# A hybrid convolution layer in Strassen-Winograd products: opening reordered, weight sums moved to VectorE, pools split by tile kind, and a rewritten end

## The chip, the cores and the metric

The kernel runs on one core of a Trainium2 chip, as one launch. Its metric is the device time of that launch in microseconds (us). TensorE (PE) multiplies matrices, VectorE (DVE) and ScalarE (ACT) work element by element, GpSimd (POOL) does so too, and SyncE (SP) issues most transfers; ACT issues some.

## The reference, cut to what matters

DEPTH is 1, so there is one layer, with the convolution mixer, on x of 2048 rows by 1024 columns, in fp32:

```python
c_act = jax.nn.silu(c)
mod = c_act @ ada_w[0] + ada_b[0]
sh_m, sc_m, g_m, sh_f, sc_f, g_f = jnp.split(mod, 6, axis=-1)
h = rms_norm(x, norm_gains[0, 0]) * (1 + sc_m) + sh_m
gate_b, gate_c, v = jnp.split(h @ conv_w_in[0], 3, axis=-1)
h = (gate_b * causal_conv3(gate_c * v, conv_w[0])) @ conv_w_out[0]
x = x + g_m * rms_norm(h, norm_gains[0, 1])
h = rms_norm(x, norm_gains[0, 2]) * (1 + sc_f) + sh_f
g, u = jnp.split(h @ ffn_w_gate_up[0], 2, axis=-1)
h = (jax.nn.silu(g) * u) @ ffn_w_down[0]
out = x + g_f * rms_norm(h, norm_gains[0, 3])
```

`rms_norm` divides a row by the root of its mean square and multiplies by a gain; 1024 is the width of the model and 2816 that of the feed-forward part.

## The kernel before, in words

Features lie on the 128 partitions and tokens along the free axis, in tiles of 128 x 512. The tokens are cut into two units of 1024, each of two halves of 512. Eight phases follow one another: in0, out0, in1, out1, gu0, down0, gu1, down1 (the digit is the unit). In each, matrix products are done in 2 x 2 blocks by Strassen-Winograd with seven products, P1 to P7, instead of eight. A product's operands are sums of blocks: of features, A11, A12, A22, S1 to S4; of weights, as `Blocks.sum` (L317) forms them. Every operand of a product is split into an upper part ("high": a cast to fp32r on ACT) and a lower part ("low": a subtraction on DVE), and one 128 x 512 step of a product is three matmuls: high weight by high feature, low weight by high feature, high weight by low feature. In the trace in0A11h and in0A11l are the high and low part of feature operand A11 of phase in0, in1b is a raw weight block of its weight group 1, in1P a weight operand, and in0P, as an output, a PSUM bank.

Nothing is scheduled by a planner. Every call goes through `Engine.emit` (L75), which keeps each engine's instructions in the order in which they are written, so all rows of the trace carry L75. The bulk of the program is a list of slots (one slot is one operand pair on PE); `schedule(slot, f)` and `later(slots, f)` put the other work between slots. `advance(step, n)` carries the weight preparation (loading blocks, summing them, casting high, forming low) up to product n. The first nine slots are not run from that list but written out by hand in `start()`, the **opening**:

- x arrives as rows (`xr`, four tiles of 128 x 1024 per half of 512 tokens) and, transposed, as features in four tiles a, c, b, d (a and b belong to token half 0, c and d to half 1; a and c hold feature blocks 0 to 3, b and d blocks 4 to 7).
- `squares` (L1009): ACT squares the rows and sums them up; `factor` (L1016): v on DVE, the power on POOL (r0p, r1p), three small DVE operations, four that build a diagonal (r0d, r1d); `spread` (L236): one PE matmul puts the factor on all partitions (r0b, r1b), ACT copies it to SBUF (r0r, r1r).
- `mult` (DVE) multiplies a feature tile by r, `shift` (ACT) applies scale mA and shift mB. For column pair q, mA comes from `scales` (DVE products of ada rows with c) and mB from `shifts` (16 PE matmuls into a row pms), `turned` (an ACT copy of the row and two PE transposes) and `fold` (four tiny DVE operations).
- `upper` and `lower` make the high and low parts, `products` issues the matmuls, `follow` the evictions from PSUM.

The products of the opening stand in the order A11 (P1), S3 (P7), A12 (P2), S2 (P6), S1 (P5), with weight groups 0, 1 and 2 in each. The features S3 need c, A12 needs b, S2 needs d.

The **end** is the second half of tokens of down1: `ready_z` (L607) is called as each of eight output tiles z is finished; `add_square` adds its squares to an accumulator (down1q). `after_down` (L875) normalises the first half and writes it, tile by tile: z becomes z times the gate mG times the factor, is added to x (tile xo) and stored. `last_half` (L920) does so for the second half, after the last matmul: PE sums the squares over the partitions (lasts), DVE and POOL take the root (lastv, lastp, lastt, lastq), DVE builds the diagonal (lastd), PE spreads it (lastb), ACT copies it (lastr), and DVE does five tiles and POOL three (5, 6, 7, scaled by mG ahead on ACT); SP stores them (tiles xl).

Of the kernel before, what the change touches and what calls it, by code (L numbers as in the profile page):

```python
# [10 lines left out]
F32 = mybir.dt.float32  # L11
F32R = mybir.dt.float32r
AF = mybir.ActivationFunctionType
ALU = mybir.AluOpType
# [32 lines left out]
def hybrid_conv_layer(  # L47
# [34 lines left out]
    sb = ctx.enter_context(tc.tile_pool(name="sb", bufs=1))  # L82
# [3 lines left out]
    def big(name, dt=F32):  # L86
        return sb.tile([P, 4, CH], dt, tag="big", bufs=NBIG, name=name)

    def raw(name):
        return sb.tile([P, CH], F32, tag="raw", bufs=NRAW, name=name)  # L90

    def pair(name):
        return sb.tile([P, 2, CH], F32, tag="wp", bufs=NWP, name=name)
# [42 lines left out]
    vt = const.tile([P, 112], F32, name="vt")  # L136
# [107 lines left out]
    def spread_later(q, name, put):  # L244
        dg = diagonal(q, name)
        yield 4
        put(spread(dg, name))
# [53 lines left out]
    class Blocks:  # L301
# [15 lines left out]
        def sum(self, op):  # L317
            b = self.b
            if op in ("P7", "P6") and "T3" not in self.summed:
                self.summed.add("T3")  # L320
                E = V if self.kind == "in" and self.opening else G
# [174 lines left out]
    class Group:  # L496
# [119 lines left out]
        def ready_z(self, c):  # L616
# [5 lines left out]
            add_square(ph.acc, tok, z, f"{ph.name}q{tok}{n}", V if ph.last and c == "21" else G, 0.5 if ph.last else 1)  # L622
            ph.tiles_done[tok] += 1
            ph.tile_ready(tok, n, z)
# [251 lines left out]
    def after_down(ph, tok):  # L876
# [10 lines left out]
        yield from spread_later(q, f"o{u}{tok}", partial(put, rb, 0))  # L887
# [16 lines left out]
        for k in range(KD):  # L904
# [6 lines left out]
            yield 2  # L911
# [4 lines left out]
    POOLS = (5, 6, 7)  # L916

    def last_half(ph):

        u, tok = ph.u, 1  # L920
        st = bank("lasts")
        for t in range(4):
            PE.matmul(st[:, t : t + 1], ph.acc[tok][:, t * P : (t + 1) * P], mean, start=True, stop=True)
        v = small(4, "lastv")
        V.tensor_scalar(v, st[:, :4], EPS, None, ALU.add)
        dg = diagonal(at_once(root(v, "last")), "last")
        b = bank("lastb")
        PE.matmul(b, one, dg[:, :CH], start=True, stop=True)
        rb = sb.tile([P, CH], F32, tag="rb", bufs=NRB, name="lastr")
        A.copy(rb, b)  # L930
        mine = [k for k in range(KD) if k not in POOLS]
        for n in range(len(mine)):
            if n < len(POOLS):
                k = POOLS[n]
                z, xt = ph.z(tok, k), ph.xt[k]
                G.tensor_tensor(z, z, rb, ALU.mult)
                G.tensor_tensor(xt, xt, z, ALU.add)
            k = mine[n]
# [4 lines left out]
        for k in POOLS:  # L943
            SP.dma_start(out_tile(u, tok, k), ph.xt[k])
        yield

    def before_last(ph):
# [4 lines left out]
        yield 1  # L952
        for k in POOLS:
            z = ph.z(1, k)
            A.activation(z, z, AF.Copy, scale=col(mG[1], k))
# [25 lines left out]
    def start():  # L981
# [34 lines left out]
        def factor(tok):  # L1016
            v = small(4, f"v{tok}")
            V.tensor_scalar(v, sq[tok], EPS, None, ALU.add)
            return diagonal(at_once(root(v, f"r{tok}")), f"r{tok}")
# [49 lines left out]
        for h in range(2):  # L1069
            A.activation(c_half[h], c_half[h], AF.Silu)  # L1070
# [4 lines left out]
        advance("blocks", 2)  # L1075
        load_scale(1)
        load_shift(1)
        load_rows(1)
# [11 lines left out]
        squares(0, range(4))  # L1090
        dg = factor(0)
# [3 lines left out]
        shifts(0)  # L1095
        for k in range(4):
            mult("a", k)
        advance("high", 2)
        turned(0)
        advance("low", 2)  # L1100
        scales(1, 0)
# [211 lines left out]
```

## Time and profile before

| | us |
|---|---|
| device time, three runs | 2041.07, 2039.4, 2040.47 |
| their median | 2040.47 |
| device time of the profiled execution | 2041.43 |
| span of the profiled execution | 2039.3 |

| engine | busy us | share of the span |
|---|---|---|
| PE | 1941.7 | 95% |
| DVE | 1444.0 | 71% |
| ACT | 855.2 | 42% |
| POOL | 691.1 | 34% |

The span is the time from the first to the last event of the profiled execution; its device time is 2.13 us more. The shares are averages over the whole span; in the page's 40 slices of 51 us each, PE is at five tenths in the first and the last, at seven in the second, and at eight or nine in all others. PE's mean granted clock over the span is 0.982 of its full 2.4 GHz; it has one other level, half of it, 1.2 GHz. Times in the trace count from the start of the span.

### The profile page before, as it was taken

The numbers are of one execution on the slowest core, as the hardware profiler recorded it, in microseconds if no ns is written. First come the engines' busy times: TensorE is split into PE (matmuls) and PEld (weight loads), VectorE is DVE, ScalarE is ACT, GpSimd is POOL, SyncE is SP. The second block draws the span as 40 slices with busy tenths as digits, with TensorE's granted clock in tenths as the row PEclk, the third lists the DMA queues.
The fourth block names the chain that finished last, engine by engine and source line by source line (L and its number), as shares of the span: only waits on it lengthen the run. The fifth ranks groups of instructions, "written<-read, shape, count | busy, mean of one in ns | idle before, by whom it ended". The sixth has DMA issues, their size and how long they took to land.

```text
span 2039.3 us, 25010 instructions
## 1 busy us (share of the span) xinstructions
PE 1941.7 (95%) x8432; PEld 1578.8 (77%) x8432; DVE 1444.0 (71%) x1878; ACT 855.2 (42%) x1382; POOL 691.1 (34%) x451
## 2 busy tenths in 40 slices
PE   5799998999989899999999999999999999999995
PEld 2578886778767778887888888887888888888884
DVE  4887887886989685699767656667767455465465
ACT  5443355632333663343333445544333333344451
POOL 0324541301542133357856431111443343311022
PEclk9899999999999999999999999999999999999998
DMA  9259959879766875477656788567646234285544
GB/s 382 74 205 352 358 203 327 322 266 347 243 212 206 300 258 175 151 232 257 224 186 218 256 280 308 196 249 258 222 162 220 94 127 132 67 326 208 203 145 136
DMA packets 206193, 463.19 MB, mean 227 GB/s; under 512 B 23024, under 2 KB 38512, under 8 KB 199152
## 3 DMA queue, kind: packets, MB, share of 16 engines
q1 hardware_dynamic: 179136, 397.49, 56.9%
q10 hardware_dynamic: 26928, 64.10, 8.3%
q8 instruction: 66, 1.08, 0.2%
q14 instruction: 63, 0.52, 0.1%
HBM read 328.33 MB, written 133.17 MB: 226 GB/s over the span
## 4 chain that ended last, share of the span: by engine, by line
PE 70%; DVE 13%; DMA 8%; ACT 4%; issue 3%; POOL 1%; SPq 0%; ACTq 0%; DVEq 0%; POOLq 0%
PE gu1P L75 20%; PE gu0P L75 16%; PE down1P L75 10%; PE down0P L75 10%; PE in0P L75 6%; PE in1P L75 5%; PE out1P L75 2%; DMA xx<-xt_d 1%; PE out0P L75 1%; DVE ada L75 1%; DMA xr<-x_d 1%; DVE zz L75 1%; DMA kgu1P<-gu1P 1%; DVE in0y L75 1%; DMA x<-xx 1%
## 5 line engine op out<-in xcount | busy, mean ns | idle before, releaser
L75 DVE TENSOR_TENSOR gu1a<-gu1P,gu1a 128x512 f32<-128x512 f32 x63 | 43.4, 690 | 93.0 <-PE gu1P L75 86.2
L75 DVE TENSOR_TENSOR gu0a<-gu0P,gu0a 128x512 f32<-128x512 f32 x63 | 43.2, 687 | 59.5 <-PE gu0P L75 54.0
L75 POOL TENSOR_TENSOR down0q<-down0q,down0q 128x512 f32<-128x512 f32 x14 | 26.0, 1859 | 152.3 <-ACT down0q L75 152.2
L75 POOL TENSOR_TENSOR down1q<-down1q,down1q 128x512 f32<-128x512 f32 x10 | 16.2, 1618 | 147.0 <-ACT down1q L75 147.0
L75 DVE CUSTOM_DVE_ANT_0 ada<-ada,c 128x512 f32<-128x512 f32 x80 | 62.5, 791 | 0.2 <-ACT c L75 0.2
L75 ACT COPY gu1a<-gu1P 128x512 f32<-128x512 f32 x42 | 24.5, 587 | 89.7 <-PE gu1P L75 78.1
L75 ACT COPY gu0a<-gu0P 128x512 f32<-128x512 f32 x42 | 24.5, 584 | 73.4 <-PE gu0P L75 65.9
L75 ACT COPY gu1g<-gu1P 128x512 f32<-128x512 f32 x24 | 14.1, 588 | 90.7 <-PE gu1P L75 85.9
L75 POOL TENSOR_TENSOR gu1a<-gu1a 128x512 f32<-128x512 f32 x11 | 19.5, 1776 | 89.8 <-DVE gu1g21s L75 24.7
L75 DVE TENSOR_TENSOR gu1g<-gu1P,gu1g 128x512 f32<-128x512 f32 x24 | 16.6, 691 | 44.9 <-ACT gu1g L75 43.6
L75 POOL TENSOR_TENSOR nq<-nq,nq 128x512 f32<-128x512 f32 x28 | 45.7, 1630 | 3.0 <-ACT nq L75 2.8
L75 ACT COPY gu0g<-gu0P 128x512 f32<-128x512 f32 x24 | 14.1, 586 | 72.6 <-PE gu0P L75 72.6
L75 POOL TENSOR_TENSOR out1q<-out1q,out1q 128x512 f32<-128x512 f32 x14 | 24.2, 1726 | 58.5 <-ACT out1q L75 58.4
L75 DVE TENSOR_TENSOR xx<-xx,zz 128x512 f32<-128x512 f32 x32 | 35.9, 1121 | 5.4 <-DMA xx<-xt_d 4.4
L75 DVE TENSOR_TENSOR gu0g<-gu0P,gu0g 128x512 f32<-128x512 f32 x24 | 16.6, 690 | 31.8 <-ACT gu0g L75 31.3
L75 POOL TENSOR_TENSOR out0q<-out0q,out0q 128x512 f32<-128x512 f32 x14 | 24.7, 1764 | 42.4 <-ACT out0q L75 42.3
L75 POOL TENSOR_TENSOR in0b<-in0b,in0b 128x512 f32<-128x512 f32 x7 | 10.7, 1533 | 79.4 <-DVE in1y L75 37.3
L75 POOL TENSOR_TENSOR gu0a<-gu0a 128x512 f32<-128x512 f32 x11 | 19.5, 1777 | 48.3 <-DVE gu0g11s L75 8.0
L75 ACT ACTIVATE gu1a<-gu1a 128x512 f32<-128x512 f32 x42 | 26.5, 633 | 15.0 <-DVE xo L75 7.7
L75 ACT ACTIVATE nq<-xx 128x512 f32<-128x512 f32 x32 | 20.2, 631 | 28.9 <-DVE xx L75 24.7
L75 ACT ACTIVATE gu0a<-gu0a 128x512 f32<-128x512 f32 x42 | 26.6, 633 | 13.5 <-DVE gu0a L75 12.2
L75 DVE TENSOR_TENSOR down2P<-down2P,down2P 128x512 fp32r<-128x512 f32 x14 | 11.1, 795 | 28.6 <-ACT down2P L75 28.6
(3209 smaller groups left out, 7014.8 us busy)
## 6 DMA issues: line engine op xcount, KB each, us to landing
ada<-ada_d SPq DMA_DIRECT2D x64, 256.0 KB, 5.2
act0A<-gu0a SPq DMA_DIRECT2D x33, 256.0 KB, 4.1
act1A<-gu1a SPq DMA_DIRECT2D x33, 256.0 KB, 3.2
ada<-ada_d SPq DMA_DIRECT2D x16, 512.0 KB, 8.9
zz<-z SPq DMA_DIRECT2D x32, 256.0 KB, 4.2
xx<-xt_d SPq DMA_DIRECT2D x32, 256.0 KB, 4.4
x<-xx ACTq DMA_DIRECT2D x32, 256.0 KB, 3.9
down0S<-act0S SPq DMA_DIRECT2D x8, 1024.0 KB, 7.4
```

What stands on the lines that cost most here:

```text
L75: return tc.keep_in_program_order(f(*args, **kwargs))
```

## The change

The change has three parts.

1. **Pools.** The pool `sb` becomes four: `bigs` (tiles of 128 x 2048), `pairs`, `raws` (128 x 512) and `sb` for the rest, and the constant `vt` is padded from 112 to 136 columns. In the allocation every tile of the first three kinds now begins, in its partition, at an address that is a multiple of 256 bytes; before, these addresses were 64 above such a multiple.
2. **Opening.** The squares of the first half of rows stand ahead of c's two activations on ACT. The rows of the second half are loaded ahead of scale and shift 1; their squares are spread (one tile before `turned(0)`, one after `fold(0)`, two after A11's first two tiles). A11's products of k = 0, 1 come before `shifts(1)`; the second factor's matmul and copy (r1b, r1r) before `turned(1)`, `fold(1)` and before A11's k = 2, 3. `scales(1, 1)` stands between POOL's power and the operations that need it. `shifts(2)` moves from before c to behind S3's products of k = 0, 1, with `turned(2)` and `shifts(3)` behind all of S3's. P7's third weight group is cast before c. A12's products are cut in two. All nine weight sums of P6 and P5 move from POOL to DVE; S1 is formed tile by tile in `start()`, and the steps of S4 and A22 are scheduled a slot earlier.
3. **End.** The last tile's square is not added to the accumulator; PE sums both (four more matmuls). All eight tiles z are scaled by mG ahead on ACT. x of five tiles (4, 5, 6, 7, 0) is put into PSUM by PE with the identity as the other operand, two tiles before the sums of squares and three after; when z has been multiplied by lastb (DVE), PE adds z into the same bank, ACT copies the sum out and issues the store. For tiles 1, 2, 3 DVE multiplies and adds. lastr and POOL's share go. The first half of tokens is written out at a closer pace (1.5 slots a tile for 2, two slots of lag for 4).

```diff
-    sb = ctx.enter_context(tc.tile_pool(name="sb", bufs=1))
+    bigs, pairs, raws, sb = (ctx.enter_context(tc.tile_pool(name=n, bufs=1)) for n in ("bigs", "pairs", "raws", "sb"))
...
         def sum(self, op):
-            b = self.b
+            b, E = self.b, V if self.opening else G
...
             if op == "P6":
-                G.tensor_tensor(b["11+"], b["12"], b["11+"], ALU.add)
+                E.tensor_tensor(b["11+"], b["12"], b["11+"], ALU.add)
             if op == "P5":
-                G.tensor_tensor(b["21"], b["21"], b["11+"], ALU.subtract)
-                G.tensor_tensor(b["11+"], b["22"], b["11+"], ALU.subtract)
+                E.tensor_tensor(b["21"], b["21"], b["11+"], ALU.subtract)
+                E.tensor_tensor(b["11+"], b["22"], b["11+"], ALU.subtract)
...
+            if ph.last and ph.tiles_done[1] == KD:
+                ph.sq = tmp("lastq")
+                A.activation(ph.sq[:, :CH], z, AF.Square)
+                scaled_z()
...
+        for k in ON_PE[:2]:
+            add_x(k)
+        for i, sq in enumerate((ph.acc[tok], ph.sq)):
+            for t in range(4):
+                PE.matmul(col(st, 4 * i + t), sq[:, t * P : (t + 1) * P], mean, start=True, stop=True)
+        for k in ON_PE[2:]:
+            add_x(k)
...
+        for k in ON_PE + tuple(k for k in range(KD) if k not in ON_PE):
             z, xt = ph.z(tok, k), ph.xt[k]
-            V.scalar_tensor_tensor(z, z, col(mG[1], k), b, ALU.mult, ALU.mult)
-            V.tensor_tensor(xt, xt, z, ALU.add)
-            SP.dma_start(out_tile(u, tok, k), xt)
...
+            V.tensor_tensor(z, z, b, ALU.mult)
+            if k in ON_PE:
+                PE.matmul(sums[k], ident, z, start=False, stop=True, skip_group_check=True)
+                A.copy(xt, sums[k])
+                A.dma_start(out_tile(u, tok, k), xt)
+            else:
+                V.tensor_tensor(xt, xt, z, ALU.add)
+                SP.dma_start(out_tile(u, tok, k), xt)
...
         squares(0, range(4))
+        for h in range(2):
+            A.activation(c_half[h], c_half[h], AF.Silu)
...
         products(0, range(2))
-        dg = factor(1)
+        scales(1, 0)
+        dg = factor(1, partial(scales, 1, 1))
+        shifts(1)
+        ps_ = bank("r1b")
+        PE.matmul(ps_, one, dg[:, :CH], start=True, stop=True)
+        turned(1)
+        rb[1] = sb.tile([P, CH], F32, tag="rb", bufs=NRB, name="r1r")
+        A.copy(rb[1], ps_)
+        fold(1)
...
         advance("sums", 5)
-        advance("high", 4)
-        rb[1] = spread(dg, "r1")
+        advance("high", 5)
...
-        shifts(2)
...
         products(3, range(2))
+        shifts(2)
+        products(3, range(2, 4))
+        turned(2)
         shifts(3)
-        products(3, range(2, 3))
-        turned(2)
-        products(3, range(3, 4))
...
-        advance("sums", 11)
         advance("high", 8)
```

On PE, between the first factor's shift row and the last A11 products, before (in0P_0, in0P_1, in0P_2 are the PSUM banks of the three weight groups; pms is the shift row, r1b the second factor spread over the partitions):

```order
MATMUL pms_262<-ada_1_158,cact 1x256 x8
MATMUL pms_262<-ident,ada_1_158 128x1 x2
MATMUL in0P_0_294<-in0A11h,in0P_243 128x512 x2
...
MATMUL in0P_2_302<-in0A11l,in2P_247 128x512
MATMUL r1b<-r1d,one 128x512
MATMUL pms_365<-ada_2_181,cact 1x256 x8
MATMUL in0P_0_401<-in0S3h,in0P_356 128x512 x2
```

and now:

```order
MATMUL in0P_2_290<-in0A11l,in2P_252 128x512
MATMUL pms_321<-ada_1_171,cact 1x256 x8
MATMUL r1b<-r1d,one 128x512
MATMUL pms_321<-ident,ada_1_171 128x1 x2
MATMUL in0P_0_282<-in0A11h,in0P_248 128x512 x2
...
MATMUL in0P_2_290<-in0A11l,in2P_252 128x512
MATMUL in0P_0_401<-in0S3h,in0P_369 128x512 x2
```

The second factor has moved from behind all 36 matmuls of A11 to behind 18 of them, with the shift row of pair 1; the shift row of pair 2 (pms with ada_2) no longer stands ahead of S3.

On DVE, from the multiplication of d to the last low part of S2, before (in0P from in0b is a low part of P6's weights; in0c and in0C there are evictions of PSUM):

```order
TENSOR_TENSOR in0d<-in0d,r1r 128x512 x4
TENSOR_TENSOR in0a<-in0d,in0e 128x512 x4
TENSOR_TENSOR in0c_11_452<-in0P_0_515,in0c_11_452 128x512
TENSOR_TENSOR in0C_11_454<-in0P_1_519,in0C_11_454 128x512
TENSOR_TENSOR in0P_543<-in0b_462,in0P_543 128x512
TENSOR_TENSOR in0S2l<-in0a,in0S2h 128x512
TENSOR_TENSOR in1P_547<-in1b_465,in1P_547 128x512
TENSOR_TENSOR in0S2l<-in0a,in0S2h 128x512
TENSOR_TENSOR in2P_551<-in2b_468,in2P_551 128x512
TENSOR_TENSOR in0S2l<-in0a,in0S2h 128x512 x2
```

and now, with P6's three sums ahead of d and P5's six behind S1's additions:

```order
TENSOR_TENSOR in0b_541<-in0b_176,in0b_541 128x512
TENSOR_TENSOR in1b_544<-in1b_180,in1b_544 128x512
TENSOR_TENSOR in2b_547<-in2b_184,in2b_547 128x512
TENSOR_TENSOR in0d<-in0d,r1r 128x512 x4
...
TENSOR_TENSOR in0S2l<-in0a,in0S2h 128x512 x2
TENSOR_TENSOR in0b_11_465<-in0P_2_560,in0b_11_465 128x512
TENSOR_TENSOR in0c<-in0c,in0d 128x512 x4
TENSOR_TENSOR in0b_199<-in0b_199,in0b_541 128x512
TENSOR_TENSOR in0b_541<-in0b_178,in0b_541 128x512
...
TENSOR_TENSOR in0S1l<-in0c,in0S1h 128x512 x4
```

The nine sums stand on DVE's queue, and none is left on POOL's.

On PE at the end, before, behind the last product (lasts are the sums of squares, lastb the factor spread out):

```order
MATMUL lasts<-mean,down1q_15761 128x1 x4
MATMUL lastb<-lastd,one 128x512
```

and now:

```order
MATMUL lastx_16080<-xl_15845,ident 128x512
MATMUL lastx_16082<-xl_15847,ident 128x512
MATMUL lasts<-mean,down1q_15787 128x1 x4
MATMUL lasts<-mean,lastq 128x1 x4
MATMUL lastx_16092<-xl_15849,ident 128x512
MATMUL lastx_16094<-xl_15851,ident 128x512
MATMUL lastx_16096<-xl_15837,ident 128x512
MATMUL lastb<-lastd,one 128x512
MATMUL lastx_16080<-down1z_15312,ident 128x512
...
MATMUL lastx_16096<-down1z_15100,ident 128x512
```

Ten matmuls with the identity have come in, two of them ahead of the sums of squares.

## Rows read from the trace of the kernel before

**Rows 1.** Busy time by stretch, core 0: us, busy and instructions by engine, clock, DMA.

```profile
31.50:43.10 11.60, 11.60 (x43) 8.53 (x43) 4.70 (x14) 6.29 (x11) 1.01 (x1) 0.85 1.03 399
43.10:54.10 11.00, 8.02 (x27) 4.19 (x26) 9.32 (x16) 6.58 (x12) 0.00 (x0) 0.79 1.02 407
...
74.05:91.50 17.45, 11.19 (x39) 7.78 (x39) 16.59 (x20) 8.41 (x14) 8.10 (x5) 0.89 0.00 0
...
138.00:200.00 62.00, 62.00 (x274) 51.29 (x274) 46.65 (x59) 22.00 (x38) 27.62 (x20) 1.00 0.97 361
```

**Rows 2.** Timeline, 7 to 45 us: start, duration, engine, operation, wait before it.

```profile
9.93 0.43 SPq L75 DMA_DIRECT2D in0a<-xt_d  x1
...
13.22 1.04 ACT L75 ACTIVATE xr<-xr 128x1024 f32<-128x1024 f32 x1
...
14.38 0.17 DVE L75 TENSOR_SCALAR v<-a 128x4 f32<-128x4 f32 x1 [9.53 <-ACT xr L75]
...
19.95 2.50 DVE L75 TENSOR_TENSOR in0a<-in0a,r0r 128x512 f32<-128x512 f32 x4 [0.34 <-ACT r0r L75]
```

**Rows 3.** Transfers issued in 2.05 to 2.7 us: count, KB each, median us to landing.

```profile
xr<-x_d SPq DMA_DIRECT2D x2, 512.0 KB, 8.0
```

**Rows 4.** Transfers issued in 0 to 60 us: count, KB each, median us to landing.

```profile
in0a<-xt_d SPq DMA_DIRECT2D x1, 1024.0 KB, 8.4
```

**Rows 5.** Chain of waits, 0 to 115 us: start, duration, engine and its work.

```profile
31.56 10.04 PE in0P L75 x36
...
43.11 0.70 DVE in0c L75
```

**Rows 6.** Timeline of PE, 42 to 64 us.

```profile
41.43 1.02 PE L75 MATMUL r1b<-r1d,one 128*128 128x512 f32 x2
...
56.52 3.61 PE L75 MATMUL pms<-ada,cact 128*1 128x256 f32 x16
```

**Rows 7.** Timeline of DVE, 43 to 110 us.

```profile
50.90 0.69 DVE L75 TENSOR_TENSOR in2P<-in2b,in2P 128x512 fp32r<-128x512 f32 x1 [1.31 <-ACT in2P L75]
...
52.71 1.46 DVE L75 TENSOR_TENSOR in0S3l<-in0e,in0S3h 128x512 fp32r<-128x512 f32 x2
...
58.82 1.75 DVE L75 TENSOR_TENSOR in2P<-in2b,in2P 128x512 fp32r<-128x512 f32 x1
60.49 1.24 DVE L75 TENSOR_TENSOR mf<-ms,ms 128x2 f32<-128x2 f32 x1
...
63.15 2.49 DVE L75 TENSOR_TENSOR in0b<-in0b,r0r 128x512 f32<-128x512 f32 x4
...
74.05 2.49 DVE L75 TENSOR_TENSOR in0d<-in0d,r1r 128x512 f32<-128x512 f32 x4
...
87.39 3.44 DVE L75 TENSOR_TENSOR in0S2l<-in0a,in0S2h 128x512 fp32r<-128x512 f32 x2
```

**Rows 8.** Groups of POOL's instructions, 54 to 92 us: busy us, mean ns of one.

```profile
L75 POOL TENSOR_TENSOR in2b<-in2b,in2b 128x512 f32<-128x512 f32 x3 | 5.0, 1683 | 0.1
```

**Rows 9.** What PE waited for, 40 to 140 us: total us, times, longest.

```profile
PE in0P L75 <- DVE in0S4l L75: 1.4, 1, 1.4
```

**Rows 10.** Timeline of all engines, 2014 to 2040 us.

```profile
2015.38 0.69 DVE L75 TENSOR_TENSOR down1z<-down1P,down1z 128x512 f32<-128x512 f32 x1 [3.95 <-PE down1P L75]
...
2017.51 1.05 PE L75 MATMUL lasts<-mean,down1q 128*128 128x1 f32 x8 [2.17 <-DVE down1q L75]
...
2021.56 2.07 PE L75 MATMUL lastb<-lastd,one 128*128 128x512 f32 x2 [3.00 <-DVE lastd L75]
...
2024.29 0.75 DVE L75 SCALAR_TENSOR_TENSOR down1z<-down1z,mG,lastb 128x512 f32<-128x512 f32 x1 [2.78 <-ACT lastr L75]
...
2034.54 0.69 DVE L75 TENSOR_TENSOR xo<-xo,down1z 128x512 f32<-128x512 f32 x1
```

**Rows 11.** Busy time by stretch at the end, as in Rows 1.

```profile
2018.97:2024.30 5.33, 2.07 (x2) 0.50 (x2) 1.37 (x8) 0.59 (x1) 1.02 (x1) 0.50 0.00 0
```

**Rows 12.** Transfers issued in 2024 to 2039 us, as in Rows 3.

```profile
out_d<-xl SPq DMA_DIRECT2D x8, 256.0 KB, 2.5
```

More of the change, by code (lines that the diff above doesn't have):

```diff
@@ L886, in after_down @@
             yield 22 + 10 * tok
-        yield from spread_later(q, f"o{u}{tok}", partial(put, rb, 0))
+        yield from spread_later(q, f"o{u}{tok}", partial(put, rb, 0), 2 if ph.last else 4)
         tiles = {}
@@ L1014, in squares, with factor @@
                 A.activation(t, t, AF.Square, scale=1.0 / 32.0, accum_out=col(sq[tok], r))
-        def factor(tok):
+        def factor(tok, meanwhile=lambda: None):
             v = small(4, f"v{tok}")
             V.tensor_scalar(v, sq[tok], EPS, None, ALU.add)
-            return diagonal(at_once(root(v, f"r{tok}")), f"r{tok}")
+            steps = root(v, f"r{tok}")
+            next(steps)
+            meanwhile()
+            return diagonal(at_once(steps), f"r{tok}")
         def shifts(q):
@@ L1162, in start @@
             lower("A12", k)
-        turned(3)
+        products(6, range(2), range(1))
         scales(3, 0)
         scales(3, 1)
+        turned(3)
         fold(3)
+        products(6, range(2), range(1, 2))
         for k in range(2, 4):
@@ L1171, in start @@
         follow(3)
-        products(6, range(4), range(2))
+        products(6, range(2, 4), range(2))
+        advance("sums", 11)
         for k in range(4):
@@ L1177, in start @@
             shift("d", k)
-            if k < 3:
-                advance("high", 9 + k)
+        follow(6, range(2))
+        products(6, range(4), range(2, 3))
+        advance("high", 11)
         for k in range(4):
@@ L1182, in start @@
             upper("S2", k)
-        follow(6, range(2))
-        products(6, range(4), range(2, 3))
-        for k in range(4):
-            if k < 3:
-                advance("low", 9 + k)
-            lower("S2", k)
-        follow(6, range(2, 3))
-        for i, step in ((9, f.s1), (9, partial(f.high, "S1")), (10, partial(f.low, "S1")), (11, f.s4),
-                        (12, partial(f.high, "S4")), (13, partial(f.low, "S4")),
-                        (14, partial(f.high, "A22")), (15, partial(f.low, "A22"))):
+            if k:
+                advance("low", 8 + k)
+                lower("S2", k - 1)
+        lower("S2", 3)
+        follow(6, range(2, 3))
+        for k in range(4):
+            V.tensor_tensor(f.t["c"][:, k, :], f.t["c"][:, k, :], f.t["d"][:, k, :], ALU.add)
+            upper("S1", k)
+        advance("sums", 14)
+        advance("high", 14)
+        for k in range(4):
+            lower("S1", k)
+        advance("low", 14)
+        for i, step in ((10, f.s4), (11, partial(f.high, "S4")), (12, partial(f.low, "S4")),
+                        (13, partial(f.high, "A22")), (14, partial(f.low, "A22"))):
             schedule(i, step)
@@ L1226, in hybrid_conv_layer @@
     schedule(first["down0"] + 22, lambda: run(mods_later((5,), 2)))
[L1227 removed]
+    schedule(first["down1"] + 73, lambda: before_last(phases[-1]))
     def multiply(s, ks=None, follow=True):
```

65 lines of the change are left out of this document (24 added, 41 removed).

## The prediction

> **What bounds the kernel now.** I read the busy time by stretch first. From 138 to 200 us PE is busy for 62.00 us of 62.00 [rows 1], and on the page PE is at eight or nine tenths in all slices but the first two and the last: the middle is a row of matmuls that the change does not shorten. A gain can come only from where PE waits, the opening and the end, and what the opening gains is carried whole to the end, since the list of slots behind it runs at PE's pace. In the stretch 43.10 to 54.10, PE works 8.02 us of 11.00 at a mean clock of 0.79, and in 74.05 to 91.50, 11.19 us of 17.45, while DVE is busy for 16.59 [rows 1]. So DVE sets the pace there. The chain of waits says the same: after A11's 36 matmuls (10.04 us) it goes over the second factor to the multiplication of c at 43.11 and then along DVE [rows 5]. At the end the timeline shows the last output of PE being added at 2015.38 and DVE working until 2035.23 on what follows [rows 10]; the span ends at 2039.3.
>
> **The pools.** New addresses alter no instruction, only how a transfer meets memory. No row of before tells addresses apart. Where PE is always busy, DMA is at 0.97 too [rows 1], and a quicker load would only wait. In the opening one load stands on the path, that of a, 8.4 us from issue to landing [rows 4]. Bounds: nothing, or some tenths of that; I take nothing. The Trainium skill (DMA: Bandwidth & Descriptors, How a descriptor splits into AXI transactions) says that a descriptor that does not start on a multiple of 256 bytes fetches unused bytes below its start and pays for them; for 2048 bytes at 64 above a multiple that is an estimated 66 beats against 64, 3%, so 0.3 us on that load, and the sum would be 0.3 us lower. No run here shows it yet.
>
> **Opening, first factor.** The last row tile is issued by about 2.6 us and takes 8.0 [rows 3], so it is there near 10.6. Its square (1.04 us [rows 2]) now waits for no activation of c, so v can start near 11.9 instead of 14.38 [rows 2]. With the same steps behind it a's multiplication could start 2.5 us before 19.95, at 17.5. But a is issued at 9.93 [rows 2] and takes 8.4 [rows 4], so it is there at 18.3. Gain: **1.6 us**; the load is what is late next. DVE's and ACT's steps to A11 follow as before, some 1.9 us sooner in all.
>
> **Second factor.** Before, its matmul stood behind all of A11 (10.04 us) [rows 5]. Now it follows half of that (5.0) and one shift row, 16 matmuls of 3.61 us in all [rows 6]. A11's first products can start near 26, after the shift of pair 0; 26 + 5.0 + 3.6 is 34.6, and the matmul of 1.02 [rows 6] and the copy give r1r near 36.4, some 6.7 us sooner. This is not the gain, since A11's other two tiles now wait for that copy on ACT and on pair 1: their low parts end near 40, then come three weight sums of 0.6 us each on DVE, and c's multiplication starts near 41.7, against 43.11 [rows 5]: **1.4 us**. If PE is at full clock all along it is 39.9; at half clock in A11's first half, 44.9. I take 41.7, nearest to the mean clock of 0.85 in that stretch [rows 1].
>
> **The stage of c and S3.** Before it lasts from 43.11 to 54.17 (52.71 + 1.46) [rows 7]. Its one long wait is the third weight group's low part at 50.90, 1.31 us behind its cast on ACT, with DVE idle between [rows 7]. The cast now stands ahead. Without that wait and the gap around it DVE's row is about 9.3 us, so S3 ends near 51.0: **3.2 us** sooner.
>
> **To b.** Before, DVE's low parts ran beside POOL's sums: 1.75 us for a 128x512 subtraction where the same one took 0.69, and 1.24 for an addition of 128x2 elements [rows 7]. Two of each cost 6.0 us; without POOL I put them at 0.6 and, as an estimate from their size, 0.2, together 1.6, so moving the sums frees 4.4 here. But ACT's copy of shift row 2 now stands ahead of the casts that these low parts need, and that row (3.61 us [rows 6]) is issued behind half of S3's products: it is ready at 54.2 if PE is at full clock and near 56.6 if not. b's multiplication then starts 2.0 to 4.5 us before 63.15 [rows 7], where the two gains added would say 7.6. The wait for the shift row takes the rest.
>
> **To S2.** From d's multiplication (74.05) to the last low part (87.39 + 3.44) are 16.8 us [rows 7]. POOL's sums in that stretch take 1683 ns each in the trace [rows 8], and the six run beside six DVE subtractions of 1.7 each: 10.2 us for 3.6. On DVE one sum is 0.6 us. Three stand ahead of d (1.8), and the rest of the stage is 17 pieces of about 0.6: 10.3 us. S2 ends **6.3 to 8.8 us** sooner. P5's six sums (3.6) now stand ahead of its low parts with S1's eight pieces (4.8): PE, which needs 6.6 us for the rest of P6, would wait up to 2.9 us there, so P5 ends 4.9 to 7.4 sooner. Behind it the wait of 1.4 us for S4 [rows 9] goes, since S4 is formed a slot earlier. That makes 6.3 to 8.8; I take off some for PE at half clock in one of the new gaps and carry **6.5 us**, with 3 and 10 as ends.
>
> **The end.** Count from the last product, 2015.36. Two copies of x into PSUM (1.02 each at full clock, as r1b [rows 6]) and two sets of four sums (1.05 a set [rows 10]) take PE to 4.15; the accumulation that stood ahead is gone. From the sums to lastb are 3.00 us [rows 10], and 0.2 for the added operation: lastb starts at 7.35, against 6.20. It takes 1.02 at full clock; before it took 2.07, at a granted clock of 0.50 [rows 10, 11]. The three other copies fit into the wait. DVE starts at 8.45 instead of 8.93 (2024.29 [rows 10]), since no copy lies between. Then five multiplications at 0.6 and three pairs at 1.3 end at 15.4; before, DVE's last addition ends at 19.87 (2034.54 + 0.69 [rows 10]). PE's five additions (5.1) end near 14.1, ACT's copy at 14.7; both kinds of stores take about 2.5 [rows 12], as before. Gain 4.5, and some tenths since the last stores are fewer at once: **4.8 us**. The closer pace of the first half costs nothing while DVE is at five tenths of its time in the last slices of the page; without that cover its last tile would fall behind the last product, as it does now.
>
> **Sum.** 6.5 + 4.8 = 11.3 from 2041.43, the profiled execution's own time: 2030.1. That execution is 0.96 above the median of 2040.47, so I forecast 2029.2.
>
> **The rivals.**
> - *The shift rows become the wait.* If PE is at half clock in A11's first half and again in S3, pms and r1b come late and ACT's casts stand behind them. For it: the mean clocks of 0.85 and 0.79 [rows 1]. Against: PE's rows are closer together there now. The opening gives 3: 2032.7.
> - *The opening gives it all.* No wait for pms, none before P5: 10 us, so 2025.7.
> - *The end at half clock.* In the trace the clock falls 3.6 us after the last product, with only small matmuls in between, and stays at 1.2 GHz [rows 11]. If it falls so again, three copies take 6.2, lastb 2.07 and five additions 10.4: lastb ends at 12.4, the additions at 23.6, the stores 27.6 after the last product, against 23.9. That is 3.7 lost instead of 4.8 gained: 2037.7. Against it: PE now works almost without a gap up to 7.2. The Trainium skill (TensorE: Matmul & The Clock Gate, Part 1: The HAM clock gate) says that the lower level is the default and that recent activity lifts it; by that the ten matmuls keep the clock up, but the wait for lastd could lose it, and this is the rule that speaks against putting additions on PE here.
> - *Slower: TensorE at 1.2 GHz both times.* PE's work from 31.50 to 54.10 is 11.60 x 0.85 + 8.02 x 0.79 = 16.2 us at full clock [rows 1]; at half it is 32.4, in a stretch that lasts 22.6: 9.8 late. The 3.2 gained there go too, so the opening loses 6.5 instead of gaining 6.5, and the end loses 3.7: 2050.7. It decides only where both happen, as one alone leaves 2042.2 or 2037.7. For it: the work is in more and smaller pieces. Against: A11's 10.04 us for 36 matmuls show mostly full clock.
>
> **How the numbers follow.** Forecast 0.62, shift rows 0.13, all of it 0.08, end at half clock 0.10, slower 0.04, and 0.03 for a wait I don't see that eats most of it. A measurement of this kernel can tell 0.2% from no change, 4.1 us: faster is below 2036.4, slower above 2044.6. The forecast and the two beside it make faster 0.84 (with a little of the end's rival), same is 0.12, slower 0.04. The range reaches from 3 us under the forecast's neighbour at 2025.7 to just short of the end's rival: 2022.5 to 2036.5.
>
> **What would show it.** In the changed profile: a's multiplication near 18.3, waiting for its load; r1r near 36; no DVE subtraction over 0.8 us before 92, and no sums on POOL; in2P of P7 without a wait; S2's last low part at 82 to 85; a wait of PE before P5 of up to 3 us, none for S4; the last product some 6.5 us sooner; PE's clock 1.00 up to lastb, DVE's work behind the last product ending 15.4 after it, and the span 18 to 20 after it. It is wrong if S2 ends later than 88, if the last product moves by less than 3 us, or if the clock is 0.50 in the additions on PE.

## The result, and the profile after

The changed kernel takes 2028.41 us (median of four runs, 2027.66 to 2029.38); the kernel before took 2040.77 in the four runs beside it. The ratio is 0.9935, 95% interval 0.9923 to 0.9948: 12.4 us faster, where 11.3 were forecast. The profiled execution took 2027.70 us with a span of 2025.9, PE busy for 1949.8 us of it.

The opening, on DVE: the timeline of the changed kernel, 36 to 110 us (start, duration, engine, operation, and in brackets the wait before it and what ended it).

```profile
40.57 1.28 DVE L75 TENSOR_TENSOR in0c<-in0c,r1r 128x512 f32<-128x512 f32 x2
...
48.40 1.46 DVE L75 TENSOR_TENSOR in0S3l<-in0e,in0S3h 128x512 fp32r<-128x512 f32 x2
...
55.75 0.69 DVE L75 TENSOR_TENSOR in0P<-in0b,in0P 128x512 fp32r<-128x512 f32 x1 [3.44 <-ACT in0P L75]
...
57.56 0.15 DVE L75 TENSOR_TENSOR mf<-ms,ms 128x2 f32<-128x2 f32 x1
...
58.09 2.48 DVE L75 TENSOR_TENSOR in0b<-in0b,r0r 128x512 f32<-128x512 f32 x4
...
70.79 2.49 DVE L75 TENSOR_TENSOR in0d<-in0d,r1r 128x512 f32<-128x512 f32 x4
...
80.16 1.29 DVE L75 TENSOR_TENSOR in0S2l<-in0a,in0S2h 128x512 fp32r<-128x512 f32 x2
```

Ahead of it, from the timeline 0 to 45 us: a's multiplication, which waits for its load, and the copy of the second factor (r1r):

```profile
18.15 2.50 DVE L75 TENSOR_TENSOR in0a<-in0a,r0r 128x512 f32<-128x512 f32 x4 [1.18 <-DMA in0a<-xt_d]
...
34.40 0.58 ACT L75 COPY r1r<-r1b 128x512 f32<-128x512 f32 x1 [0.69 <-PE r1b L75]
```

Against [rows 5, 7], c's multiplication starts 2.5 us sooner (40.57 for 43.11), S3's last low part ends 4.3 sooner (49.86 for 54.17), b starts 5.1 sooner (58.09 for 63.15), d 3.3 sooner (70.79 for 74.05), and S2's last low part ends 9.4 sooner (81.45 for 90.83). The addition of 128x2 that took 1.24 us beside POOL takes 0.15. A new wait of 3.44 us on DVE stands ahead of P2's low parts.

How far PE has come shows at the last product of the first three weight groups, A22 with in2P; the next row belongs to in3P. First the timeline of PE before, then after:

```profile
124.95 0.39 PE L75 MATMUL in0P<-in0A22l,in2P 128*128 128x512 f32 x1
125.18 0.61 PE L75 MATMUL in0P<-in0A11h,in3P 128*128 128x512 f32 x2
```

```profile
117.30 0.39 PE L75 MATMUL in0P<-in0A22l,in2P 128*128 128x512 f32 x1
117.53 0.62 PE L75 MATMUL in0P<-in0A11h,in3P 128*128 128x512 f32 x2
```

So the opening gains **7.65 us** (125.34 to 117.69). I call this point the end of the opening. At the other end, busy time by stretch (us; busy and instructions of PE, PEld, DVE, ACT, POOL; clock, DMA share, GB/s), cut behind the last product, where DVE begins on lastb, and where DVE ends. Before:

```profile
2015.36:2024.29 8.93, 3.13 (x10) 1.47 (x10) 4.17 (x12) 1.22 (x2) 1.02 (x1) 0.70 0.00 1
2024.29:2035.23 10.94, 0.00 (x0) 0.00 (x0) 10.73 (x12) 0.00 (x0) 9.39 (x6) 0.50 0.46 172
2035.23:2039.30 4.07, 0.00 (x0) 0.00 (x0) 0.01 (x1) 0.00 (x0) 0.00 (x0) 0.50 0.56 184
```

After:

```profile
2006.04:2013.60 7.56, 7.20 (x28) 3.63 (x27) 2.37 (x10) 1.35 (x2) 1.02 (x1) 1.00 0.00 0
2013.60:2020.70 7.10, 4.56 (x10) 1.81 (x10) 6.95 (x11) 2.92 (x5) 0.00 (x0) 1.00 0.46 153
2020.70:2025.90 5.20, 0.00 (x0) 0.00 (x0) 0.00 (x0) 0.00 (x0) 0.00 (x0) 0.83 0.59 196
```

PE works through the wait for the factor (7.20 us of 7.56), its clock stays at 1.00 to the last addition, and the stretch behind the last product falls from 23.9 to 19.9 us. Behind DVE's last operation it grew, from 4.07 to 5.20. The eight stores of 256 KB there, issued over 4.9 us, took longer to land than the 2.5 of before [rows 12] (transfers issued in 2013 to 2026 us):

```profile
out_d<-xl ACTq DMA_DIRECT2D x5, 256.0 KB, 3.3
out_d<-xl SPq DMA_DIRECT2D x3, 256.0 KB, 3.8
```

With 7.65 and 4.1 the two ends give 11.8 us of the 13.4 by which the spans differ. The rest lies between. Counted from the end of the opening to the last product that stretch lasted 1890.0 before and 1888.4 after; in the fourteen profiled executions of this study it lies anywhere from 1884.8 to 1893.8, in kernels whose programs differ there in the last few slots at most, so such a difference tells nothing of one kernel. The spread arises in the phases in0 to gu0: from the last product of gu0 to the last product of all, the fourteen take 841.5 to 841.7 us.

### The profile page after: what moved, and what is told of

Read it like the earlier page. It is cut to its first block, busy times and chain, and to the rows that moved or that the text cites. A ratio compares the mean times of both kernels' runs of the same rounds, so it can differ in the third digit from the quotient of the medians.

```text
span 2025.9 us, 25058 instructions
## 1 busy us (share of the span) xinstructions
PE 1949.8 (96%) x8460; PEld 1583.4 (78%) x8460; DVE 1436.3 (71%) x1894; ACT 862.8 (43%) x1394; POOL 668.6 (33%) x436
## 4 chain that ended last, share of the span: by engine, by line
PE 72%; DVE 13%; DMA 7%; issue 4%; ACT 3%; SPq 0%; POOL 0%; ACTq 0%; POOLq 0%; DVEq 0%
PE gu1P L75 20%; PE gu0P L75 16%; PE down0P L75 10%; PE down1P L75 9%; PE in0P L75 7%; PE in1P L75 6%; PE out0P L75 2%; PE out1P L75 2%; DVE zz L75 1%; DMA xr<-x_d 1%; DMA xx<-xt_d 1%; DVE xx L75 1%; DVE ada L75 1%; DVE gu0a L75 1%; DVE in1y L75 0%
## 5 line engine op out<-in xcount | busy, mean ns | idle before, releaser
L75 POOL TENSOR_TENSOR out1q<-out1q,out1q 128x512 f32<-128x512 f32 x14 | 24.1, 1724 | 59.1 <-ACT out1q L75 59.0
L75 POOL TENSOR_TENSOR in3b<-in3b,in3b 128x512 f32<-128x512 f32 x4 | 9.6, 2389 | 77.9 <-DMA in3b<-w_in_d 63.9
L75 ACT ACTIVATE gu1a<-gu1a 128x512 f32<-128x512 f32 x42 | 26.6, 633 | 14.7 <-DVE xo L75 7.7
```

The lines of the kernel that those rows point to most:

```text
L75: return tc.keep_in_program_order(f(*args, **kwargs))
```

## The experiments

The numbers of all runs, from the timelines and results; "c" and "b" are the starts of their multiplications, "opening" is its end as above, "end" the time from the last product to the end of the span. Ratios are to runs of the kernel before on the same chip in the same session (its medians there: 2041.36 beside e1 to e4, 2041.24 beside e5 to e8, 2042.60 beside e9 to e11, 2040.71 beside e12). Single executions spread over some 8 us in these sessions (before: 2037.8 to 2046.3 in the first), so the marks of a trace tell apart what medians can't.

| kernel | median us | ratio, 95% | c | b | opening | end |
|---|---|---|---|---|---|---|
| before | 2040.77 | | 43.11 | 63.15 | 125.34 | 24.0 |
| changed | 2028.41 | 0.9935 (0.9923 to 0.9948) | 40.57 | 58.09 | 117.69 | 19.9 |
| e1 pools alone | 2040.12 | 0.9996 (0.9986 to 1.0007) | 42.20 | 62.27 | 124.18 | 24.0 |
| e2 opening alone | 2035.55 | 0.9975 (0.9962 to 0.9988) | 42.55 | 60.07 | 118.68 | 24.1 |
| e3 end alone | 2037.76 | 0.9983 (0.9972 to 0.9994) | 43.09 | 63.12 | 125.05 | 19.8 |
| e4 changed, old pools | 2030.88 | 0.9947 (0.9934 to 0.9960) | 41.03 | 58.55 | 118.09 | 19.9 |
| e5 sums on POOL | 2032.56 | 0.9957 (0.9945 to 0.9968) | 41.90 | 62.32 | 121.67 | 19.8 |
| e6 second factor late | 2034.52 | 0.9961 (0.9948 to 0.9973) | 45.60 | 65.49 | 125.97 | 19.8 |
| e7 shift row 2 early | 2026.06 | 0.9921 (0.9907 to 0.9935) | 40.75 | 54.74 | 114.34 | 19.9 |
| e8 P6's sums in the gap | 2028.30 | 0.9933 (0.9921 to 0.9945) | 42.28 | 59.79 | 117.49 | 19.9 |
| e9 copies behind lastb | 2033.53 | 0.9957 (0.9943 to 0.9970) | 42.11 | 59.62 | 119.23 | 22.9 |
| e10 end on DVE alone | 2033.62 | 0.9951 (0.9937 to 0.9965) | 41.99 | 59.51 | 119.12 | 21.7 |
| e11 P5 group by group | 2027.79 | 0.9927 (0.9914 to 0.9939) | 43.19 | 57.19 | 121.08 | 19.1 |
| e12 e7, P5's low part, end | 2027.53 | 0.9934 (0.9920 to 0.9949) | 42.32 | 56.32 | 114.92 | 19.0 |

### The parts apart: e1 to e4

```diff
e1, on before (taken back on the changed kernel in e4):
+    bigs, pairs, raws, sb = (... for n in ("bigs", "pairs", "raws", "sb"))
+    vt = const.tile([P, 112 + 24], F32, name="vt")[:, :112]
e2: the opening's part of the change alone, e3: the end's part alone
```

> The kernel before with its pools split and vt padded, nothing else. Theory (addresses are worth nothing, since no load but a's stands on the path): within 1 us of before, 2040.8, and the stretch 14 to 60 us of the opening as before to 0.3 us. Rival (the some 1.1 us that the changed kernel gains beyond its opening and its end come from cheaper transfers): 1 to 3 us faster, 2038 to 2040, with the product of phase in1 starting sooner.

> The changed kernel with the pools and vt as before. Theory: no difference beyond 1 us, 2028.4. Rival (addresses count): 1 to 3 us slower than the changed kernel, 2029.5 to 2031.5.

e1's median is 1.2 us below that of before beside it, and the interval, from 2.9 us faster to 1.4 slower, takes in no change. Its opening ends 1.2 us sooner than before's; in this execution PE's clock did not fall in A11, as it did in that of before, and c starts 0.9 us sooner behind the same program. e4 lies 0.4 us behind the changed kernel at every mark from c on, and what it does carry of the addresses shows at a's load: a's multiplication, which waits for that load, starts at 18.14 to 18.31 in the nine executions with the new opening and new addresses, and at 18.39 and 18.46 in e2 and e4 with old ones. About 0.2 us, by a load that is on the path. This is e4's row:

```profile
18.46 2.49 DVE L75 TENSOR_TENSOR in0a<-in0a,r0r 128x512 f32<-128x512 f32 x4 [1.36 <-DMA in0a<-xt_d]
```

In the opening the rival of 1 to 3 us is out. By time it is not: e4's median, 2030.88, lies in the rival's range, though its interval overlaps that of the changed kernel. The stretch between, where such a gain would have to be, takes 1889.1 us in the mean of the four executions with old addresses and 1888.4 in that of the ten with new ones, which is no difference beside a spread of 9.

> The kernel before with the new opening, the old pools and the old end. Theory: the opening alone gives what the last product of phase in0 shows, 8.2 us, carried whole: 2032.5. Rival (part of it hangs on the new addresses): at most 6.5 us, 2034 or more, with low parts in the opening later than in the changed kernel.

> The kernel before with the new end alone. Theory: the stretch behind the last product falls from 23.9 us to 19.9, so 4.1 us faster, 2036.7; granted clock 1.00 up to the last addition on PE. Rival (the closer pace of the first half of tokens takes some of it back before the last product): the last product later than before by 1 us or more, 2038 or more.

The opening alone ends at 118.68, 6.7 us sooner than before, and the end alone takes 19.8, 4.2 us less. The parts add up as far as can be told: by the medians 5.8, 3.6 and 1.2 (pools) against 12.4 for the whole and 10.5 for e4, by the traces 6.7 and 4.2 against 11.8. e2 missed its 2032.5 and landed in its rival's range (2034 or more). But e4, with old addresses too, ends its opening within 0.4 us of the changed kernel, so addresses are not what e2 lacks there: c starts 2 us later than in the changed kernel. Busy time by stretch of the changed kernel and of e2 shows why (columns as above):

```profile
25.00:30.00 5.00, 4.88 (x20) 3.39 (x21) 3.99 (x11) 3.50 (x7) 1.19 (x1) 1.00 1.03 424
...
36.00:41.00 5.00, 4.20 (x10) 3.08 (x11) 3.54 (x6) 3.58 (x7) 0.00 (x0) 0.66 1.03 417
```

```profile
25.00:30.00 5.00, 4.51 (x12) 3.30 (x13) 3.67 (x10) 3.87 (x7) 0.82 (x1) 0.66 1.04 415
...
36.00:41.00 5.00, 2.77 (x10) 1.69 (x10) 1.71 (x4) 3.36 (x5) 0.00 (x0) 0.92 1.04 410
```

The same instructions stand on PE in both. In the changed kernel's execution the clock fell in A11's second half, in e2's in its first, ahead of the second factor. Of the eleven profiled executions with the new opening, the three with the low clock in A11's second half only start c from 40.57 to 41.03, and the seven others with the second factor early from 41.90 to 43.19 (e6 has it late). The forecast of 41.7 lies between the two. So part of the changed kernel's 7.65 us is the place of its low clock: e9 and e10, whose opening is the same program, end it at 119.23 and 119.12 and gain 6.1 and 6.2.

e3's last product comes 3.5 us later than that of before (2018.83 for 2015.34), which is the sign of its rival. But the closer pace of the first half is at work in the last phase, down1, and there PE has no gap to lose, before (first row) or in e3 (second):

```profile
1820.00:2015.30 195.30, 195.30 (x864) 161.16 (x862) 105.37 (x125) 86.63 (x125) 17.45 (x11) 1.00 0.57 197
...
1820.00:2018.80 198.80, 198.80 (x881) 164.40 (x880) 111.24 (x131) 91.53 (x130) 20.50 (x13) 1.00 0.59 201
```

From the last product of gu0 on both take 841.7 us; e3's delay arose ahead of that, and the rival is out.

### The opening's steps: e5, e6, e8

```diff
e5, in Blocks.sum, for P6 and P5:
-                E.tensor_tensor(...)
+                G.tensor_tensor(...)
e6:
-        ps_ = bank("r1b") ... A.copy(rb[1], ps_)      (behind shifts(1))
+        rb[1] = spread(dg, "r1")                      (behind all of A11)
```

> The changed kernel with the nine sums of P6 and P5 on POOL again, at the places where they now stand. Theory (POOL's sums slow DVE's two-input operations beside them and are themselves slow): DVE operations of 128x512 over 1.2 us in the stretch 69 to 95, S1's products 4 to 6 us later than 89.69, the last A22 product of the first three weight groups near 121.5 instead of 117.69, time 2032. Rival (off DVE they are hidden): within 1 us of 117.69 or sooner, since DVE has 5.4 us less to do.

The end of the opening is at 121.67, as expected to 0.2 us, but with c at 41.90; relative to c it is 2.7 us later than in the changed kernel, since of the 7.3 us by which S1's products start later (97.03, where 4 to 6 were expected) PE gets some back behind them. The median is 4.1 higher. Groups of DVE's and POOL's instructions by shape, 69 to 95 us, of e5:

```profile
L75 DVE TENSOR_TENSOR in0a<-in0d,in0e 128x512 f32<-128x512 f32 x4 | 4.8, 1225 | 0.0
L75 DVE TENSOR_TENSOR in0S2l<-in0a,in0S2h 128x512 fp32r<-128x512 f32 x4 | 4.7, 1204 | 0.3 <-ACT in0S2h L75 0.3
...
L75 POOL TENSOR_TENSOR in1b<-in1b,in1b 128x512 f32<-128x512 f32 x2 | 3.3, 1646 | 1.3 <-ACT in0S2h L75 1.3
```

and of the changed kernel:

```profile
L75 DVE TENSOR_TENSOR in0S2l<-in0a,in0S2h 128x512 fp32r<-128x512 f32 x4 | 2.7, 686 | 0.3 <-ACT in0S2h L75 0.3
L75 DVE TENSOR_TENSOR in0a<-in0d,in0e 128x512 f32<-128x512 f32 x4 | 2.6, 682 | 0.0
```

The same subtractions take 1204 to 1225 ns in the mean, and 682 to 686 without POOL's sums. One by one, from the timeline of e5, beside a sum that POOL starts at 78.85, and at 82.29, when POOL had none:

```profile
78.98 1.70 DVE L75 TENSOR_TENSOR in0S2l<-in0a,in0S2h 128x512 fp32r<-128x512 f32 x1 [0.26 <-ACT in0S2h L75]
...
82.29 0.68 DVE L75 TENSOR_TENSOR in1P<-in1b,in1P 128x512 fp32r<-128x512 f32 x1
```

From d's multiplication to S2's last low part e5 takes 16.0 us, the changed kernel 10.7. Nine sums of 0.6 us on DVE's own queue are cheaper than the same nine off it.

> The changed kernel with the second factor's matmul and copy behind all of A11 again. Theory (it sets when c starts): c's multiplication at 44.8 instead of 40.57, and 3 to 4 us of that are left at the last A22 product, 121. Rival (DVE waits 3.44 us behind shift row 2 anyway, so a later c is absorbed there): b's multiplication within 1 us of 58.09, the last A22 product within 1 us of 117.69.

From the timeline of e6 on DVE:

```profile
45.60 1.29 DVE L75 TENSOR_TENSOR in0c<-in0c,r1r 128x512 f32<-128x512 f32 x2 [3.92 <-ACT r1r L75]
...
63.15 0.69 DVE L75 TENSOR_TENSOR in0P<-in0b,in0P 128x512 fp32r<-128x512 f32 x1 [5.81 <-ACT in0P L75]
```

Against the changed kernel's execution c starts 5.0 us later and the opening ends 8.3 later, but part of this is the clock, which fell there only in A11's second half. In e9 it fell where it did in e6 (0.50 from 26 to 29 us in both); against e9 (42.11 and 119.23) c is 3.5 us later and the end of the opening 6.7. Nothing of it is absorbed. DVE's wait ahead of P2's low parts grows from 3.44 to 5.81, since shift row 2 stands behind half of S3's products, and these now run in part at 1.2 GHz. The second factor is worth more than the 3 to 4 us expected, and the rival is out.

```diff
e8:
         advance("high", 8)
+        advance("sums", 11)
         advance("low", 8)
...
-        advance("sums", 11)                           (ahead of d)
```

> The changed kernel with P6's three sums on DVE moved from ahead of d into the wait behind shift row 2. Theory (they cost 1.8 us where they stand, and nothing there): b as in the changed kernel, 58.09, d at 69.0 instead of 70.79, the last A22 product at 115.9, time 2026.6. Rival (behind S2, PE and not DVE sets the pace): S2's last low part sooner, but the last A22 product within 0.5 us of 117.69.

d follows c by 28.40 us where it took 30.22: the 1.8 us are gained. c itself started 1.7 us later in this execution, and so d is at 70.68 and the end of the opening at 117.49. Measured from c the gain is there, in the median (2028.30) it is not visible.

### What holds b: e7

```diff
e7:
         f.t["e"] = big(f"{ph.name}e")
+        shifts(2)
...
         products(3, range(2))
-        shifts(2)
+        turned(2)
         products(3, range(2, 4))
-        turned(2)
```

> The changed kernel with shift row 2 issued on PE directly behind A11, and its turning in the middle of S3's products. Theory (what holds b back is this row, ahead of ACT's copies and casts): DVE's wait of 3.44 us goes, b's multiplication at 55.2 instead of 58.09, S2's last low part at 78.6, the last A22 product near 114.8, time 2025.5. Rival (the row delays S3's products by 3.6 us and so its own and the next evictions): b within 1 us of 58.09.

Where it was, the row was read 4.3 us after ACT was free for it. ACT's timeline of the changed kernel, and below it that of e7:

```profile
53.40 0.36 ACT L75 COPY ada<-pms 1x256 f32<-1x256 f32 x1 [4.27 <-PE pms L75]
...
55.10 0.62 ACT L75 CAST in0P<-in0b 128x512 fp32r<-128x512 f32 x1
```

```profile
49.22 0.36 ACT L75 COPY ada<-pms 1x256 f32<-1x256 f32 x1
...
50.91 0.61 ACT L75 CAST in0P<-in0b 128x512 fp32r<-128x512 f32 x1
```

DVE's wait is gone, b starts at 54.74 and the opening ends at 114.34, 3.4 us sooner, each within 0.5 us of what was expected. S3's products start 2.9 us later (46.62 for 43.77) and still end 2.2 sooner (55.51 for 57.69), since the row no longer stands among them. The median is 2026.06 (expected 2025.5), the lowest of all versions here; its interval overlaps that of the changed kernel, so the 3.4 us are shown in the opening and not yet in the time.

### P5's wait: e11, e12

```diff
e11:
-        advance("sums", 14), advance("high", 14), lower S1 0 to 3, advance("low", 14)
+        for n in range(3): sums 12 + n, high 12 + n, two of lower S1 (n < 2), low 12 + n
e12: the order of the changed kernel, with advance("low", 12) behind lower S1 1
both: shift row 2 as in e7, and at the end one copy of x ahead of the sums of squares, three behind, one behind lastb
```

> Shift row 2 early (as in the run before), P5's sums, casts and low parts on DVE group by group between S1's low parts instead of all six sums first, and at the end one copy of x ahead of the sums of squares, three behind, one behind lastb. Theory: b at 54.7; PE no longer waits 1.3 us for P5's first low part, S1's products begin 2 us sooner relative to S2's end, and S4's low part is what holds PE next, so the last A22 product near 113; the end 19.5: time 2024.5. Rival (DVE's row up to S4's low part is the bound, whatever its order): the last A22 product within 0.5 us of 114.34.

Both theories missed. PE waits 6.82 us before S1's first product, in place of 2.10 and 1.31 in the changed kernel, and then works at 1.2 GHz; the end of the opening is at 121.08. What ends the wait is not DVE but a copy on ACT. Timeline of PE in the changed kernel, 78 to 110, then in e11, 70 to 112:

```profile
89.69 0.50 PE L75 MATMUL in0P<-in0S1h,in0P 128*128 128x512 f32 x1 [2.10 <-ACT in0c L75]
...
91.51 0.50 PE L75 MATMUL in0P<-in0S1h,in0P 128*128 128x512 f32 x1 [1.31 <-DVE in0P L75]
```

```profile
93.48 1.22 PE L75 MATMUL in0P<-in0S1h,in0P 128*128 128x512 f32 x2 [6.82 <-ACT in0c L75]
```

And ACT in the changed kernel, 80 to 93, then in e11, 80 to 95:

```profile
88.53 0.62 ACT L75 CAST in2P<-in2b 128x512 fp32r<-128x512 f32 x1 [0.70 <-DVE in2b L75]
89.06 0.58 ACT L75 COPY in0c<-in0P 128x512 f32<-128x512 f32 x1
```

```profile
92.32 0.62 ACT L75 CAST in2P<-in2b 128x512 fp32r<-128x512 f32 x1 [3.58 <-DVE in2b L75]
92.85 0.58 ACT L75 COPY in0c<-in0P 128x512 f32<-128x512 f32 x1
```

P5 adds to the PSUM bank that P6 filled, so its first matmul waits for ACT to copy that bank out (in0c). In ACT's row the copy stands behind P5's three casts, and the last of these waits for the last of DVE's sums. e11 moved that sum back behind the low parts, and with it the copy.

> Shift row 2 early; all six sums of P5 first, as in the changed kernel, with P5's first low part between S1's second and third; the end of the run before (one copy of x ahead, three behind, one behind lastb). Theory (P5's first product waits first for ACT's copy of a PSUM bank, which stands behind the casts that wait for these sums, and then for its low part): the wait of 6.82 us in the run before is 2.1 again, the one of 1.3 us behind it goes, and against the run with shift row 2 alone the last A22 product is 1.2 us sooner, 113.1, if c starts at 40.75 as there; the end 19.1 us; time 2024.1. Rival (S4's low part holds PE as long): the last A22 product as far behind c as with shift row 2 alone, 73.6 us, time 2025.3.

With the sums first again the wait is 2.03 us, and the one of 1.31 behind it is gone. Timeline of PE in e12:

```profile
87.93 1.41 PE L75 MATMUL in0P<-in0S1h,in0P 128*128 128x512 f32 x2 [2.03 <-ACT in0c L75]
```

From c to the end of the opening are 72.6 us, where e7 has 73.6 and the changed kernel 77.1. The end takes 19.0, 0.8 us less. c started late in this execution (42.32), so the mark itself is 114.92 and not 113.1. Its median, 2027.53, is not to be told from e7's or the changed kernel's.

### The end: e9, e10

```diff
e9:
-        for k in ON_PE[2:]: add_x(k)                  (ahead of lastb)
+        for k in ON_PE[2:]: add_x(k)                  (behind lastb)
e10:
-    ON_PE = (4, 5, 6, 7, 0)
+    ON_PE = ()
```

> The changed kernel with the last three copies of x into PSUM behind lastb's matmul instead of in the wait ahead of it. Theory (these copies keep PE at work in the wait, and so the clock up): the granted clock falls to 0.50 before the additions on PE, lastb takes 2.1 us, three copies 1.9 each and five additions 1.9 each, and the stretch behind the last product is 26 to 28 us instead of 19.9. Rival (the wait is too short for the clock to fall): clock 1.00 to the last addition, three copies at 0.94 less the 0.8 us that PE waits there now, 22 us.

Busy time by stretch of e9, from its last product on (columns as above):

```profile
2010.21:2015.70 5.49, 3.39 (x20) 2.35 (x19) 1.50 (x6) 1.35 (x2) 1.02 (x1) 1.00 0.00 0
2015.70:2022.50 6.80, 5.85 (x7) 2.50 (x8) 4.58 (x11) 0.00 (x0) 0.00 (x0) 0.50 0.00 0
2022.50:2033.10 10.60, 5.04 (x12) 1.90 (x10) 3.25 (x5) 2.93 (x5) 0.00 (x0) 0.98 0.58 199
```

The clock fell to 1.2 GHz 5.5 us after the last product, inside a wait of 3.05 us without a matmul, so the rival is out; lastb took 2.07 us and the three copies 4.7. But PE was at full clock again for the additions, so the price is 3.0 us and not the 6 to 8 that I expected. The copies in the wait do keep the clock up; what they save is lastb and themselves.

> The changed kernel with no tile on PE and ACT at the end: DVE multiplies and adds all eight, SP stores them. Theory: eight pairs of 1.3 us on DVE in place of the 7.1 us that it works behind lastb now, so 3.4 us more, and lastb at 1.2 GHz, 0.9 more, less 1.0 since lastb starts sooner without copies ahead of it: a stretch behind the last product of 23 us, the clock at 0.50 from 3.5 us after the last product on. Rival (the stores set the end, 2 MB on their way): within 1 us of 19.9.

It is 21.7 us, between the two. The clock fell, 4.7 us after the last product (3.5 expected), and DVE ends 18.3 us after the last product instead of 14.7. But from there to the end of the span are 3.3 us where the changed kernel takes 5.2: its eight stores of 256 KB are issued over 9.6 us, not 4.9. So of the 3.7 us that DVE saves by sharing with PE, the stores take 1.9 back. By the ratios e9 and e10 are 4.5 and 3.3 us slower than the changed kernel, each give or take some 4; the traces show 3.0 and 1.8 of it at the end and 1.5 and 1.4 in the opening, where their programs are the same and the low clock fell earlier.

## Why the prediction was right, point by point

The forecast, 2029.2 against 2028.41, stood on two terms, 6.5 and 4.8; measured they are 7.65 and 4.1. The sum came out closer than its parts, and that is luck: the two misses have opposite signs, and of the first 1.4 to 1.5 us are the place of the low clock in this execution, without which the opening gains 6.1 to 6.2 (e9, e10).

- **What bounds the kernel.** Right. From 138 to 200 us PE is again busy for all of it. That the opening's gain is carried whole fits, with the last product 9.3 us sooner, but is shown only to within the spread of the stretch between.
- **Pools at nothing.** Right in the opening, but for a's load, which came some 0.2 us sooner; by time it is not settled, since e1 leaves room from 2.9 us faster to 1.4 slower and e4's median is 2.5 above the changed kernel's. By the rule of the Trainium skill (DMA: Bandwidth & Descriptors, How a descriptor splits into AXI transactions) I had an estimate of 0.3 for that load. The measured 0.2 leans to it, but the rule speaks of bytes fetched and these are addresses written to, so no run shows that it is the cause. The term is too small for the sum.
- **First factor.** Forecast 1.6 us, with a's load next; measured 1.8 (18.15), the wait being for that load.
- **Second factor and c.** r1r was forecast at 36.4 and is there at 34.98; c at 41.7, measured 40.57 in this execution and 41.90 to 43.19 in most others, by where the low clock falls. So the 1.4 us for c against before are 2.5 here and 1.2 at most in those. That the move counts is shown by e6: without it, the clock falling in the same place, c is 3.5 us later and the end of the opening 6.7.
- **c and S3.** 9.29 us against a forecast of 9.3.
- **The way to b.** The step that the shift row would take back part of the gain was right, and e7 shows it: without it b comes 3.4 us sooner still. I gave 2.0 to 4.5, the upper end for PE at full clock through S3; it was at full clock, and the gain is 5.1. The 0.6 beyond comes from c, which was 1.1 sooner than forecast: from c to b it takes 17.5 us here and in the four other executions with the same work in between (e2, e4, e9, e10), whose gains are 3.1 to 4.6.
- **S2.** From d's multiplication to the last low part, forecast 10.3, measured 10.66. By my terms (16.8 less 10.3, less 1.8 for P6's sums ahead of d) this stage gives 4.7, but the range of 6.3 to 8.8 holds only 4.3 for it, a slip that the 10.66 happens to make good: measured, it is 4.3. The gain of 9.4 is beyond my 8.8 because b was. e5 shows that the contention is its cause (16.0 us with the sums on POOL).
- **P5.** A wait of up to 2.9 us was forecast, measured 3.4 in two pieces. But the cause that I gave, DVE's sums ahead of the low parts, is only the second piece (1.31); the first (2.10) is a copy of PSUM on ACT behind casts that wait for the sums. I had not looked at what else stands in ACT's row there. The working also takes only 1.4 us off the gain for this wait, and does not say why. The wait for S4 went, as forecast.
- **The end.** DVE begins on lastb 7.60 us behind the last product (8.45 forecast) and ends at 14.65 (15.4). So DVE's part gave 5.2, where 4.5 were forecast. What I mis-sized is the last term, stores of about 2.5 as before and some tenths gained "since the last stores are fewer at once". They are more at once: eight come within 4.9 us, take 3.3 and 3.8, and cost 1.1 us. e10 bears it out: eight over 9.6 us, and 3.3 us behind DVE instead of 5.2.
- **The rivals.** Shift rows as the wait: the low clock in A11's first half is there in most executions and costs 1.4 to 1.5 us of the opening (e9, e10), not 3.5; S3 at low clock, its other condition, is there in e6 alone. The end at 1.2 GHz did not happen; e9 and e10 show that lastb falls to it as soon as the copies are not in the wait. With the rule of the Trainium skill (TensorE: Matmul & The Clock Gate, Part 1: The HAM clock gate), that activity lifts the clock, all three traces agree: 1.00 at lastb with the copies in the wait, 0.50 without. The slower case needed the low clock in the opening and at the end; it was there for part of A11 only (0.66 from 36 to 41 us).

What stays open is the stretch between: 1884.8 to 1893.8 us in fourteen executions, which no run here was made to explain. All of that spread lies ahead of the last product of gu0. In the changed kernel the table of PE's waits puts the largest there in in1, out0 and out1 (5.4, 5.6 and 3.3 us), each behind an operation of ACT.

## What to carry to other kernels

A second elementwise engine is not a free place for work: where two engines slow each other, moving sums onto the busier one can shorten its stage. When an operation is moved, read every in-order row that it stands in, not only the one that it loads: twice here a small copy on ACT set the pace, once ahead of the casts and waiting for PE (a shift row), once behind casts that wait for DVE (a PSUM bank). And a wait of the matrix engine at the end is a place for copies that have to be made anyway; count the stores behind it, which bunch when the work ahead of them gets faster.

## What the runs showed of the hardware that was not expected

The same row of instructions on PE met its low clock in different places from one execution to the next: between 24 and 31 us in seven executions with the second factor early and at 37 to 41 alone in three, which moved c by up to 2.6 us. And at the end of e9 the clock came back from 0.50 to 1.00 while PE worked without a gap on lastb and the copies, so that the additions ran at full clock again: 4.45 us for five, against 4.56 in the changed kernel, where it never fell.
